# Inverses of 16 x 16 diagonal blocks on their way through memory: the transposed ones first, and by GpSimd's queue

## The chip, the cores and the metric

The kernel runs on one core of a Trainium2 chip. The metric is device time in microseconds of one execution. The core has five engines that run their own instruction streams and wait for each other by semaphores: TensorE (PE, with its weight loads as PEld), VectorE (DVE), ScalarE (ACT), GpSimd (POOL) and SyncE (SP). SP issues most transfers; ACT and POOL can issue some as well. Transfers of all queues are moved by 16 DMA engines.

## The reference

Two layers of a decoder trunk over 512 tokens of width 1024, float32. Each layer is a SwiGLU block, a mixer and a second SwiGLU block, each with a scaled residual and a layer norm. The mixer has three parts: differential attention, stick-breaking attention, and a gated delta rule with 4 heads of width 128. The change touches the delta rule only:

```python
l_mat = jnp.where(strict, jnp.einsum('bhncd,bhned->bhnce', k_beta, k) * decay, 0.0)
t_mat = l_mat + jnp.eye(CHUNK, dtype=jnp.float32)
sol = lax.linalg.triangular_solve(t_mat, rhs, left_side=True, lower=True, unit_diagonal=True)
u, w = sol[..., :dv], sol[..., dv:]
```

Per head and chunk a lower triangular matrix with ones on its diagonal is solved against; a scan over the chunks follows.

## The kernel before

Activations lie with features on the partitions and the 512 tokens along the free side. Every float32 matrix product of the projections is three matmuls of rounded parts (lines 103 to 105, `mm3`): high part of the weights by high part of x, high by low, low by high. Weights come in tiles of 512 KB (`wraw`, line 81) and are split by ScalarE (`whi`, line 89) and by VectorE or POOL (`wlo`, line 90).

The delta rule uses chunks of 128 tokens instead of the 64 of the reference, 4 chunks (NC) by 4 heads. `triangle` (line 660) makes the triangular matrices LT of a head and writes them to a scratch in memory (`scr[0]`, line 675). `base` (line 688) inverts the 16 x 16 blocks on their diagonals, all heads at once: it reads the blocks from the scratch so that each of the 128 partitions holds one whole block (U), and VectorE eliminates in 15 steps (lines 700 and 702, Y the inverse). Then Y and its transpose are written into two other scratches, each block to its place on the diagonal of a matrix that was filled with zeros at the start (line 1127, issued by POOL): `scr[1]` for the plain inverses, `scr[2]` for the transposed ones. `diagonals` (line 403) gives the addresses: 128 blocks of 16 runs of 16 numbers, 64 bytes each. From there each head's matrices come back to SBUF as whole 128 x 128 matrices, XT from `scr[1]` (line 708) and X from `scr[2]` (line 710), 256 KB each.

`double` (line 713) merges blocks of 16 into blocks of 32 for one head: a product of the masked LT with X (line 718), a copy out of PSUM by ScalarE (line 720), a product with XT (line 723), a subtraction into XT by VectorE (line 724), transposes by TensorE (line 727), and a copy into X by ScalarE (line 728). `join` goes on to 64 and 128. `outputs` (line 866) runs the scan over the chunks. Beside this chain the mixer runs attention units (`attend`, line 884; their score matmuls are lines 880 and 881, their value matmuls 909) and the projections (`full_tile`, line 345). The projection of queries and keys copies its result about in SBUF by many small transfers (`stack`, line 524, tile name `kqv`), issued by SP.

The program is written as a list of such steps; a scheduler then sets the order of the instructions on each engine from the dependencies and its own estimates of durations, so an edit in one step can move instructions of others. Each engine runs its list in order; a transfer whose data isn't ready holds up whatever stands behind it in the list of the engine that issues it.

Of the kernel before, what the change touches and what calls it, by code (L numbers as in the profile page):

```python
# [396 lines left out]
def slabs(t, h):  # L397

    a = t[:]
    return bass.AP(tensor=a.tensor, offset=a.offset + h * NC * SLAB, ap=[[P, P], [SLAB, NC], [1, P]])  # L400


def diagonals(t, h, n):

    a = t[:]
    return bass.AP(tensor=a.tensor, offset=a.offset + h * NC * SLAB, ap=[[SB * P + SB, n * NC * P // SB], [P, SB], [1, SB]])
# [20 lines left out]
def mixer(g, l):  # L427
    nc = g.nc
# [121 lines left out]
    n = 2 * HEADS  # L550
    p = pav.tile([P, T], F32, name="pt")
# [134 lines left out]
    XT, X = [None] * HEADS, [None] * HEADS  # L686

    def base(h0, n):

        q = n * NC * P // SB  # L690
        U = mp.tile([q, SB, SB], F32, name="blk")
        nc.sync.dma_start(out=U, in_=diagonals(g.scr[0], h0, n))
        Y = mp.tile([q, SB, SB], F32, name="blk")
        tt = mp.tile([q, SB * SB // 4], F32, name="blkt", bufs=1)
        nc.gpsimd.memset(Y, 0.0)
        nc.gpsimd.memset(Y.rearrange("p i j -> p (i j)")[:, 0:SB * SB:SB + 1], 1.0)
        for k in range(SB - 1, 0, -1):
            w = SB - k
            t = tt[:, 0:k * w].rearrange("p (i j) -> p i j", j=w)
            nc.vector.tensor_tensor(out=t, in0=U[:, 0:k, k:k + 1].to_broadcast([q, k, w]),  # L700
                                    in1=Y[:, k:k + 1, k:SB].to_broadcast([q, k, w]), op=ALU.mult)
            nc.vector.tensor_tensor(out=Y[:, 0:k, k:SB], in0=Y[:, 0:k, k:SB], in1=t, op=ALU.subtract)
        nc.sync.dma_start(out=diagonals(g.scr[1], h0, n), in_=Y)
        nc.vector.tensor_copy(out=U, in_=Y.rearrange("p i j -> p j i"))
        nc.sync.dma_start(out=diagonals(g.scr[2], h0, n), in_=U)
        for h in range(h0, h0 + n):
            XT[h] = mp.tile([P, NC, P], F32, name="XT", bufs=4)
            nc.sync.dma_start(out=XT[h], in_=slabs(g.scr[1], h))
            X[h] = mp.tile([P, NC, P], F32, name="inv", bufs=10)
            nc.sync.dma_start(out=X[h], in_=slabs(g.scr[2], h))  # L710


    def double(h):
# [136 lines left out]
    def triangles():  # L850

        for h in range(HEADS):
            products(h)
        norms(0, HEADS)
        for h in range(HEADS):
            triangle(h)
        base(0, HEADS)
# [401 lines left out]
```

## Time and profile before

| | |
|---|---|
| time, median of 3 runs | 2249.18 us (2244.98 to 2249.8) |
| the profiled execution | 2250.16 us, its span 2248.4 us |
| granted TensorE clock, mean | 0.985 |
| TensorE busy | 2138.2 us (95%) |
| VectorE, ScalarE, POOL busy | 1169.6, 907.9, 377.5 us |

The span goes from the first to the last instruction. A busy TensorE is not a TensorE at its peak, since matmuls are pipelined. A row of a timeline gives the start in us from the span's start, the duration, the engine, the line, the operation, output and inputs with their shapes, the count, and in brackets the idle time of the engine before it with what ended it. SPq stands for the instructions by which SP issues transfers; a transfer lands later than its issue ends.

### The profile page before, as it was taken

The page shows a single profiled execution, that of the slowest core. Times are in us where ns is not written, and L with a number is a line of the kernel's source. Part 1 is how long each engine was busy: PE and PEld are TensorE (multiplying, and loading weights), DVE is VectorE, ACT ScalarE, POOL GpSimd, SP SyncE. Part 2 cuts the span into 40 slices and gives each one's busy share as a digit, 9 for nine tenths or more (in the row PEclk, how much of TensorE's full clock was granted, in tenths as well). Part 3 has the DMA queues.
Part 4 walks back from the last instruction along what each step waited for, and adds up shares of the span by engine and source line. Part 5 has one row for each costly group of instructions (what it writes and reads, how often), then busy time and mean ns, then how long its engine had stood idle before and what let it go on. Part 6 is the DMA issues. An engine that isn't in the chain of part 4 may idle for free. (4 is left out here: it accounts for less than half of the span.)

```text
span 2248.4 us, 30132 instructions
## 1 busy us (share of the span) xinstructions
PE 2138.2 (95%) x11382; PEld 1782.6 (79%) x11382; DVE 1169.6 (52%) x2363; ACT 907.9 (40%) x1801; POOL 377.5 (17%) x327
## 2 busy tenths in 40 slices
PE   8999999999798999999999999999987989999997
PEld 7888889777677888888888888897776768888886
DVE  4533436386578833343663334263774788333426
ACT  4333324575464533332443333245753535333313
POOL 1100011426204400000130000023461234000010
PEclk9999999999899999999999999999998999999998
DMA  6423323514512233332333333234144123333322
GB/s 190 125 94 95 98 75 104 139 40 122 129 58 72 84 109 94 94 94 75 116 109 95 94 94 94 66 104 131 57 133 109 48 85 94 95 96 100 95 66 94
DMA packets 90898, 217.32 MB, mean 97 GB/s; under 512 B 21968, under 2 KB 36336, under 8 KB 90752
## 3 DMA queue, kind: packets, MB, share of 16 engines
q1 hardware_dynamic: 82848, 187.47, 27.5%
q10 hardware_dynamic: 6912, 25.17, 3.8%
q0 software_dynamic: 992, 2.75, 0.7%
q8 instruction: 90, 1.47, 0.3%
q14 instruction: 56, 0.46, 0.1%
HBM read 193.83 MB, written 6.83 MB: 89 GB/s over the span
## 5 line engine op out<-in xcount | busy, mean ns | idle before, releaser
L89 ACT CAST whi<-wraw 128x512 fp32r<-128x512 f32 x692 | 421.4, 619 | 959.4 <-PE pd L104 755.1
L90 DVE TENSOR_TENSOR wlo<-wraw,whi 128x512 fp32r<-128x512 f32 x580 | 431.0, 751 | 658.6 <-ACT whi L89 647.4
L103 PE MATMUL pd<-x,whi 128*128 128x512 f32 (+1 forms) x1920 | 726.7, 380 | 12.9 <-ACT x L1177 6.2
L105 PE MATMUL pd<-x,wlo 128*128 128x512 f32 (+1 forms) x1920 | 728.3, 380 | 3.2 <-DVE wlo L90 3.2
L104 PE MATMUL pd<-x,whi 128*128 128x512 f32 (+1 forms) x1920 | 727.7, 379 | 1.6 <-POOL x L231 1.3
L103 PEld LDWEIGHTS pd<-x,whi 128*128 128x128 f32 x1920 | 365.8, 191 | 77.5 <-ACT x L1177 6.2
L105 PEld LDWEIGHTS pd<-x,wlo 128*128 128x128 f32 x1920 | 366.2, 191 | 67.4 <-DVE wlo L90 3.4
L104 PEld LDWEIGHTS pd<-x,whi 128*128 128x128 f32 x1920 | 366.2, 191 | 66.8 <-POOL x L231 3.0
L103 PE MATMUL pd<-hhi,whi 128*128 128x512 f32 (+1 forms) x880 | 307.7, 350 | 0.0
L104 PE MATMUL pd<-hlo,whi 128*128 128x512 f32 (+1 forms) x880 | 307.7, 350 | 0.0
L105 PE MATMUL pd<-hhi,wlo 128*128 128x512 f32 (+1 forms) x880 | 307.3, 349 | 0.0
L168 POOL TENSOR_TENSOR lt<-lt 128x512 f32<-128x512 f32 x26 | 38.9, 1497 | 1065.3 <-ACT lt L165 1065.3
L103 PEld LDWEIGHTS pd<-hhi,whi 128*128 128x128 f32 x880 | 165.5, 188 | 24.4
L105 PEld LDWEIGHTS pd<-hhi,wlo 128*128 128x128 f32 x880 | 165.4, 188 | 24.1
L104 PEld LDWEIGHTS pd<-hlo,whi 128*128 128x128 f32 x880 | 165.5, 188 | 24.1
L90 POOL TENSOR_TENSOR wlo<-wraw,whi 128x512 fp32r<-128x512 f32 x112 | 150.2, 1357 | 138.7 <-ACT whi L89 70.1
L259 DVE TENSOR_TENSOR lt<-pd,lt 128x512 f32<-128x512 f32 x88 | 60.4, 689 | 111.9 <-PE pd L105 110.7
L231 POOL TENSOR_TENSOR x<-x 128x256 fp32r<-128x256 f32 x60 | 45.1, 753 | 162.5 <-ACT x L229 132.7
L134 POOL TENSOR_TENSOR x<-x 128x512 f32<-128x512 f32 x48 | 70.9, 1522 | 0.0
L261 DVE TENSOR_TENSOR hlo<-lt,hhi 128x512 fp32r<-128x512 f32 x88 | 67.0, 765 | 6.3
L165 ACT ACTIVATE lt<-x 128x256 f32<-128x256 f32 (+1 forms) x58 | 29.7, 512 | 95.8 <-DVE x L163 95.5
L568 DVE SCALAR_TENSOR_TENSOR kqv<-pd,conv,kqv 128x511 f32<-128x511 f32 (+2 forms) x72 | 53.5, 743 | 20.1 <-ACT kqv L566 18.9
(309 smaller groups left out, 2287.9 us busy)
## 6 DMA issues: line engine op xcount, KB each, us to landing
wraw<-in_w SPq DMA_DIRECT2D x308, 512.0 KB, 3.5
wraw<-in_w ACTq DMA_DIRECT2D x48, 512.0 KB, 3.6
kqv<-kqv SPq DMA_DIRECT2D x128, 64.0 KB, 2.0
kqv<-kqv SPq DMA_DIRECT2D x48, 128.0 KB, 4.7
scr<-zero POOLq DMA_DIRECT2D x2, 1032.0 KB, 11.1
x<-in_xT SPq DMA_DIRECT2D x8, 256.0 KB, 5.5
scr<-inv SPq DMA_DIRECT2D x8, 256.0 KB, 2.7
XT<-scr SPq DMA_DIRECT2D x8, 256.0 KB, 4.8
```

Source lines behind the costliest of these rows:

```text
L89: nc.scalar.copy(out=hi, in_=r)
L90: (eng or self.eng or nc.vector).tensor_tensor(out=lo, in0=r, in1=hi.bitcast(F32), op=ALU.subtract)
L103: nc.tensor.matmul(out=out, lhsT=whi, rhs=xhi, start=first, stop=False)
L104: nc.tensor.matmul(out=out, lhsT=whi, rhs=xlo, start=False, stop=False)
L105: nc.tensor.matmul(out=out, lhsT=wlo, rhs=xhi, start=False, stop=last)
L134: i = g.nc.gpsimd.tensor_tensor(out=t, in0=xhi.bitcast(F32), in1=xlo.bitcast(F32), op=ALU.add)
L165: nc.scalar.activation(out=sq[:, r], in_=t[:, r], func=AF.Square)
L168: eng.tensor_tensor(out=self.acc2[:, r], in0=self.acc2[:, r], in1=sq[:, r], op=ALU.add)
L231: eng.tensor_tensor(out=xlo[:, r], in0=t[:, r], in1=xhi[:, r].bitcast(F32), op=ALU.subtract)
L259: nc.vector.tensor_tensor(out=sg, in0=pu, in1=sg, op=ALU.mult)
L261: nc.vector.tensor_tensor(out=hlo, in0=sg, in1=hhi.bitcast(F32), op=ALU.subtract)
L568: nc.vector.scalar_tensor_tensor(out=y[:, s:], in0=p[:, :T - s], scalar=wc[:, 3 - s:4 - s], in1=y[:, s:], op0=ALU.mult, op1=ALU.add)
```

## The change

The copy that makes the transposed inverses (U) now stands ahead of both writes in the code, the transposed write comes first and is issued by POOL, and so are the four loads of X. The plain write and the four loads of XT stay on SP.

```diff
-        nc.sync.dma_start(out=diagonals(g.scr[1], h0, n), in_=Y)
         nc.vector.tensor_copy(out=U, in_=Y.rearrange("p i j -> p j i"))
-        nc.sync.dma_start(out=diagonals(g.scr[2], h0, n), in_=U)
+        nc.gpsimd.dma_start(out=diagonals(g.scr[2], h0, n), in_=U)
+        nc.sync.dma_start(out=diagonals(g.scr[1], h0, n), in_=Y)
         for h in range(h0, h0 + n):
             XT[h] = mp.tile([P, NC, P], F32, name="XT", bufs=4)
             nc.sync.dma_start(out=XT[h], in_=slabs(g.scr[1], h))
             X[h] = mp.tile([P, NC, P], F32, name="inv", bufs=10)
-            nc.sync.dma_start(out=X[h], in_=slabs(g.scr[2], h))
+            nc.gpsimd.dma_start(out=X[h], in_=slabs(g.scr[2], h))
```

After the change the copy has line 703, POOL's write 704 and SP's write 705; the loads keep 708 and 710.

In the difference below, of SP's list at the end of `base`, rows with a minus stand in the list of before, rows with a plus in the list now (of the minus rows, those from the third head on).

```order
-L708 DMA XT<-scr_99 128x4x128
-L710 DMA inv<-scr_100 128x4x128
-L708 DMA XT<-scr_99 128x4x128
-L710 DMA inv<-scr_100 128x4x128
-L524 DMA kqv<-kqv 32x512 x18
+L705 DMA scr_99<-blk 128x16x16
+L524 DMA kqv<-kqv 32x512 x3
+L708 DMA XT<-scr_99 128x4x128 x4
+L524 DMA kqv<-kqv 32x512 x17
 L81 DMA wraw<-in_w 128x1024 x153
```

The four loads of X have left SP's list, so that the four of XT follow each other, and the small copies of `stack` follow directly.

In POOL's list at the same place, with `blk` the block tile U and `inv` X:

```order
 L696 MEMSET blk 128x16
 L90 TENSOR_TENSOR wlo<-wraw,whi 128x512 x2
+L704 DMA scr_100<-blk 128x16x16
+L710 DMA inv<-scr_100 128x4x128 x4
 L995 TENSOR_TENSOR kqv<-x,kqv 128x256 x8
 L134 TENSOR_TENSOR x<-x 128x512 x8
```

The write and the loads stand behind two splits of weights and ahead of the splits of the mixer's outputs.

In TensorE's list around the first L718, the first product of `double` (`pd` is a projection's PSUM tile):

```order
 L103 MATMUL pd<-x,whi 128x512
 L104 MATMUL pd<-x,whi 128x512
+L105 MATMUL pd<-x,wlo 128x512
+L103 MATMUL pd<-x,whi 128x512
+L104 MATMUL pd<-x,whi 128x512
+L105 MATMUL pd<-x,wlo 128x512
+L103 MATMUL pd<-x,whi 128x512
 L718 MATMUL pa<-inv,lt 128x128 x4
-L105 MATMUL pd<-x,wlo 128x512
-L103 MATMUL pd<-x,whi 128x512
-L104 MATMUL pd<-x,whi 128x512
-L105 MATMUL pd<-x,wlo 128x512
```

Five matmuls of a projection have moved from behind L718 to ahead of it; further on the order of the doubling and the attention units differs in many places.

## Rows read from the trace of the kernel before

**Rows 1.** The page, its head.
```profile
span 2248.4 us, 30132 instructions
```

**Rows 2.** The waits: waiting engine and line, releaser; us, times, longest.
```profile
PE pa L718 <- DMA inv<-scr: 8.2, 2, 4.8
```

**Rows 3.** The timeline of SP's issues, layer 0, end of `base`.
```profile
593.89 0.37 SPq L703 DMA_DIRECT2D scr<-blk  x1
594.37 0.88 SPq L705 DMA_DIRECT2D scr<-blk  x1
...
597.86 0.53 SPq L708 DMA_DIRECT2D XT<-scr  x1
598.49 0.48 SPq L710 DMA_DIRECT2D inv<-scr  x1
...
603.31 11.93 SPq L524 DMA_DIRECT2D kqv<-kqv  x18
```

**Rows 4.** The timeline of VectorE, the same place.
```profile
593.86 0.37 DVE L704 COPY blk<-blk 128x256 f32<-128x256 f32 x1
594.15 0.68 DVE L511 SCALAR_TENSOR_TENSOR kqv<-pd,kqv 128x512 fp32r<-128x512 f32 x1
605.93 0.69 DVE L90 TENSOR_TENSOR wlo<-wraw,whi 128x512 fp32r<-128x512 f32 x1 [11.10 <-ACT whi L89]
```

**Rows 5.** The chain that ended last, layer 1: start, us, what.
```profile
1707.84 4.03 DMA scr<-blk
```

**Rows 6.** The timeline of TensorE, layer 0, around the first L718.
```profile
601.92 2.04 PE L718 MATMUL pa<-inv,lt 128*128 128x128 f32 x8 [3.36 <-DMA inv<-scr]
603.61 0.77 PE L105 MATMUL pd<-x,wlo 128*128 128x512 f32 x1
604.18 0.63 PE L103 MATMUL pd<-x,whi 128*128 128x512 f32 x1
604.61 0.63 PE L104 MATMUL pd<-x,whi 128*128 128x512 f32 x1
...
606.47 1.13 PE L723 MATMUL pa<-XT,inv 128*128 128x128 f32 x8
```

**Rows 7.** The timeline of TensorE, layer 1, the same place.
```profile
1715.30 2.05 PE L718 MATMUL pa<-inv,lt 128*128 128x128 f32 x8 [4.80 <-DMA inv<-scr]
...
1720.98 1.20 PE L723 MATMUL pa<-XT,inv 128*128 128x128 f32 x8
```

**Rows 8.** The timeline of TensorE, layer 0, later heads.
```profile
613.04 1.06 PE L718 MATMUL pa<-inv,lt 128*128 128x128 f32 x8
613.85 0.42 PE L880 MATMUL psc<-kqv 128*128 128x384 f32 x1
...
617.26 1.06 PE L718 MATMUL pa<-inv,lt 128*128 128x128 f32 x8
```

**Rows 9.** The timeline of ScalarE, layer 0.
```profile
605.28 0.62 ACT L89 CAST whi<-wraw 128x512 fp32r<-128x512 f32 x1 [12.33 <-PE pd L104]
605.80 0.58 ACT L720 COPY inv<-pa 128x512 f32<-128x512 f32 x1
```

**Rows 10.** The page's transfers: issuer, count, KB each, median us from issue to landing.
```profile
scr<-zero POOLq DMA_DIRECT2D x2, 1032.0 KB, 11.1
...
inv<-scr SPq DMA_DIRECT2D x8, 256.0 KB, 5.2
...
scr<-blk SPq DMA_DIRECT2D x4, 128.0 KB, 3.5
...
lt<-in_mask POOLq DMA_DIRECT2D x1, 128.0 KB, 2.3
```

**Rows 11.** The timeline of POOL, the second zero fill.
```profile
53.26 1.13 POOL L1127 DMA_DIRECT2D scr<-zero  x1 [11.51 <-issue]
```

**Rows 12.** The timeline of POOL after 593.8, layer 0.
```profile
665.83 1.56 POOL L995 TENSOR_TENSOR kqv<-x,kqv 128x256 fp32r<-128x256 f32 x2 [72.03 <-ACT kqv L994]
```

**Rows 13.** Stretches: us, engines' busy time, granted clock, DMA share, GB/s.
```profile
602.00:603.00 1.00, 1.00 (x5) 1.00 (x6) 0.00 (x0) 0.00 (x0) 0.00 (x0) 0.50 1.11 300
```

More of the change, by code (lines that the diff above doesn't have):

```diff
@@ L702, in base @@
             nc.vector.tensor_tensor(out=Y[:, 0:k, k:SB], in0=Y[:, 0:k, k:SB], in1=t, op=ALU.subtract)
+        nc.vector.tensor_copy(out=U, in_=Y.rearrange("p i j -> p j i"))
+        nc.gpsimd.dma_start(out=diagonals(g.scr[2], h0, n), in_=U)
         nc.sync.dma_start(out=diagonals(g.scr[1], h0, n), in_=Y)
-        nc.vector.tensor_copy(out=U, in_=Y.rearrange("p i j -> p j i"))
-        nc.sync.dma_start(out=diagonals(g.scr[2], h0, n), in_=U)
         for h in range(h0, h0 + n):
```

## The prediction

> **What bounds the kernel now.** First the page's head: the span is 2248.4 us [rows 1]. The profiled execution took 2250.16 us, so 1.76 us lie around the span; the median of the three runs shown is 2249.18, 0.98 below this execution. The sum is made against 2250.16 and the 0.98 is taken off at the end.
>
> Second, the view of waits: TensorE waits 8.2 us in all, in two places and at most 4.8 us, for the transfer "inv<-scr", which is X of head 0 (line 710) [rows 2]. These two places, one in each layer, are where the change works. Third, the timelines around the first. VectorE ends the copy into U at 594.23 and SP issues its write at 594.37 [rows 3, 4]. That write lands 4.03 us after its issue (row of layer 1) [rows 5], in layer 0 at 598.40; SP issues the load of X at 598.49 [rows 3], and TensorE starts the first product of `double` (L718) at 601.92, after 3.36 us without work [rows 6]. In layer 1 L718 starts at 1715.30 after 4.80 us [rows 7].
>
> After that a chain sets the pace: L718, ScalarE's copy L720, L723, VectorE's subtraction L724, L727, and the next head. The L718 of two successive heads stand 4.22 us apart (613.04 and 617.26) [rows 8]. So what counts is when the first L723 can start: 606.47 and 1720.98, that is 4.55 and 5.68 us after L718 [rows 6, 7]. In between TensorE does nine matmuls of the projection, and ScalarE's L720 stands behind a cast that waits until 605.28 for a TensorE matmul (L104), ending a wait of 12.33 us [rows 9].
>
> **The change part by part.**
>
> *Swapped order and the copy first.* VectorE's instructions keep their order: in the kernel before, the copy already stood directly behind the last L702, and the plain write was issued beside it. Cost 0. What the copy's write gains is that it no longer stands behind the plain write on SP: 594.37 less 594.23 is 0.14 us, and some of this is the signal. I take 0.05. The load gains as little: SP had issued it 0.09 us after the landing (598.49 less 598.40). SP's issue time, 0.37 and 0.53 us for the two instructions ahead [rows 3], was thus almost all hidden.
>
> In sentences of their own: the Trainium skill, "DMA: Bandwidth & Descriptors", section "Issuing engines are not separate DMA queues", says that several issuing engines save only the time of issuing. Going by that rule alone the move is worth at most these 0.23 us a layer; the trace agrees as far as it shows the issue hidden.
>
> *The write by POOL's queue (128 x 16 runs of 64 bytes).* No row shows this write on POOL. Low end: the plain write, first in its queue, lands after about 3.0 us (the page's median for the four writes is 3.5 [rows 10], and the second is at 4.0); lower still would be POOL's load of 128 KB in 2.3 us [rows 10], which has few runs. High end: POOL's zero fill, also 128 x 16 runs but of 516 bytes, landed after 11.1 us (median of two) [rows 10]; its issue took 1.13 us [rows 11]. Between 2.3 and 11.1 I take 4.2: the same bytes at the same addresses are SP's 3.0, POOL's issue is longer by about 0.8 (1.13 less 0.37), and the two writes now run side by side where they ran one behind the other, 0.4 more. POOL is free: its last subtraction (L90) ends at 593.8 and the next work before was at 665.83, after 72.03 us of idling [rows 12], so what stands behind the POOL transfers (L995) does not feel them. The write then lands at 594.32 plus 4.2, 598.5, against 598.40: 0.1 late.
>
> In sentences of their own: VectorE runs L511 from 594.15 to 594.83, over the start of POOL's issue, and then nothing until 605.93 [rows 4]. The Trainium skill, "SBUF — State Buffer", section "SBUF: two separate sides", warns that a VectorE instruction in a two-port mode locks GpSimd out, so that it cannot write descriptors and its DMA starts late; it gives 3.1 us against 0.62 beside a copy. Whether L511 is such an instruction no run here shows. If it is, the lock ends with it: 0.5 us a layer, and the gain of the sum below would be 1.0 smaller.
>
> *The load by POOL's queue.* Before, from issue to L718 3.43 us (598.49 to 601.92) [rows 3, 6], behind one XT load. Now all four XT loads, 1 MB, go out on SP from about 597, as soon as the plain write has landed. At the 300 GB/s of the busy stretch [rows 13] they fill 3.5 us, to about 601.5, and X of head 0, issued at 598.6, shares the engines with the last two. Low end 2.3 (POOL's 128 KB load [rows 10]); high end 5.2 (the median of the eight X loads, most of them issued behind others) [rows 10]. I take 3.6, near the row before, since before it also shared. X arrives at 602.2 instead of 601.9: about 0.3 late, 0.6 for two layers.
>
> *The order of TensorE.* The scheduler now puts five matmuls of the projection, 13 instead of 8, ahead of L718, and leaves four instead of nine between L718 and L723. The five find TensorE idle: at 0.43 each (604.18 to 604.61 [rows 6]) they are 2.15 us, inside the 3.36 and 4.80 us of waiting. The cast that L720 stands behind then runs before L718, because the matmul that it waits for is among the five (it was the third after L718). New distance L718 to L723, at the slow clock of this stretch (granted 0.50 from 602 to 603, that is 1.2 GHz [rows 13]): 1.69 to the next matmul (601.92 to 603.61), then 0.57 and three times 0.43, together 3.55. ScalarE's L720 needs 0.58 of this and is hidden; if that cover goes, L720 and its handoff add up to 0.6. Gain: 4.55 less 3.55 is 1.00 in layer 0, 5.68 less 3.55 is 2.13 in layer 1, together 3.1. The same 17 matmuls are done at L723 as before, so nothing is only put off to there.
>
> *What follows.* XT of head 0 is issued about a microsecond earlier than 597.86 and is needed last at L723: no cost. The copies of keys and queries behind the loads on SP (L524, 18 of them from 603.31 [rows 3]) start about 3 us earlier. TensorE's order of the doubling changes, too, but that stretch is paced by the chain of 4.22 us; later the attention work already used as filler is missing. I take 0 for all this, with 3 us either way.
>
> **The sum.** Less 3.1, plus 0.6: less 2.5 us. 2250.16 becomes 2247.7, and by the 0.98 a median of 2246.7.
>
> **The rivals.**
>
> *Slower: POOL's write of 2048 small runs lands late.* For it: the only POOL transfer with as many runs took 11.1 us, and a second one like it did not start its issue until 11.51 us after the first [rows 11]. Against: it carried eight times the bytes, beside weight loads. Every microsecond that the write lands later than assumed delays L718, and all behind it, once a layer. With 10 us instead of 4.2 it is 2 x 5.8 less 2.5, or 9.1 slower: 2258.3. It decides from (2.5 + 4.5) / 2 above 4.2, so a landing after 7.7 us is slower than a measurement's doubt; at 5.4 us the gain is gone.
>
> *Faster: the clock stays up.* Before, L718 took 1.69 us to the next matmul at 1.2 GHz and later 0.81 (613.04 to 613.85 [rows 8]), about half; the matmuls' 0.43 would be 0.22. With the wait shortened by five matmuls TensorE may come to L718 at 2.4 GHz: 0.88 plus 4 x 0.21, some 1.7 a layer, 3.4 in all: 2243.3. Against: in layer 1 2.6 us or more of the wait stay.
>
> *Faster, by transfers: POOL's write and load land like its plain loads.* The 2.3 us of [rows 10] instead of 4.2 and 3.6 is 3.2 us a layer; X cannot be used before TensorE is through with its 13 matmuls (598.56, where the wait of 3.36 began, plus 2.15 is 600.7), so 1.5 us a layer count: 3.0 in all, 2243.7. In a sentence of its own: the Trainium skill, "DMA: Bandwidth & Descriptors", section "Anatomy of one DMA — SWDGE (gpsimd) path", fits a DMA by 2.0 us plus its bytes at 436 GB/s, which agrees with the 2.3 but not with the 11.1 of the zero fill (it would give 4.4).
>
> *No effect: the gain is lost behind.* The fill-in work that now stands ahead of L718 is missing in the stretch of the state scan, and the chain's lead is eaten there: 2249.
>
> **How the numbers follow.** About 0.2% of the time, 4.5 us, is what a measurement of this kernel tells from no change. Chances: forecast 0.32, lost behind 0.18, slow write 0.23, clock 0.16, fast transfers 0.11. The forecast (less 2.5) and the loss (0) lie within 0.2%; a little of the forecast's spread of 3 us goes beyond on the fast side, and the two fast rivals lie 5.5 to 5.9 below and just beyond the bound. So faster 0.30, same 0.46, slower 0.24. The range goes from both fast rivals together (2240) to close to the slow write (2257).
>
> **What would show it.** Right: in the profile after, 13 matmuls ahead of L718, the wait before L718 down to some 1.5 us in layer 0 (598.56 plus 2.15 is 600.7, X at 602.2), L723 about 3.6 us behind L718, and POOL's write landing some 4 us after its issue. Wrong: a landing above 6 us, a wait before L718 as long as before or longer, or the same time of L723 and then more idling of TensorE between 608 and 700 us.

## The result, and the profile after

The changed kernel takes 2276.26 us (median of 6 runs, 2272.78 to 2284.49) against 2249.46 for the kernel before (6 runs): a ratio of 1.0125 over the runs (1.0119 by the two medians), 95% interval 1.0112 to 1.0138. It is 26.8 us slower by the medians. 2246.7 was forecast, with a range of 2240 to 2257. The profiled execution is the slowest of the six (2284.49), so lengths of stretches are compared here, not times from the start. Its head answers to [rows 1]:

```profile
span 2282.7 us, 30147 instructions
```

The waits (us, times, longest). The first row answers to [rows 2]; the second is ScalarE's copy of a scan step's result out of PSUM, 22.4 us in all and at most 4.0 before:

```profile
PE pa L718 <- DMA inv<-scr: 14.2, 2, 8.0
ACT o L840 <- PE pa L798: 50.7, 12, 15.7
```

The place that the prediction was about, layer 0, answers to [rows 3, 4 and 6]: VectorE's copy, the issues of SP and POOL, and TensorE.

```profile
595.69 0.38 DVE L703 COPY blk<-blk 128x256 f32<-128x256 f32 x1
595.72 0.37 SPq L705 DMA_DIRECT2D scr<-blk  x1
596.49 1.22 POOL L704 DMA_DIRECT2D scr<-blk  x1 [0.86 <-DVE blk L703]
598.72 2.66 SPq L708 DMA_DIRECT2D XT<-scr  x4
601.75 2.99 POOL L710 DMA_DIRECT2D inv<-scr  x4 [4.04 <-DMA scr<-blk]
607.95 2.04 PE L718 MATMUL pa<-inv,lt 128*128 128x128 f32 x8 [8.00 <-DMA inv<-scr]
611.50 1.86 PE L723 MATMUL pa<-XT,inv 128*128 128x128 f32 x8
```

POOL issues the first load of X only at 601.75, three microseconds after SP began to issue the four loads of XT, and L718, which waits for X, starts 6.2 us later. The wait before L718 is 8.0 us, although five more matmuls stand ahead of it. L723 follows after 3.55 us, as forecast. Layer 1 answers to [rows 7]:

```profile
1740.30 2.05 PE L718 MATMUL pa<-inv,lt 128*128 128x128 f32 x8 [6.17 <-DMA inv<-scr]
1743.85 1.48 PE L723 MATMUL pa<-XT,inv 128*128 128x128 f32 x6
```

That is some 4 us a layer, less what L718 to L723 gives back. The greater part lies further on, in the state scan (L779 is a product of each of its steps, with XT and the scaled values). Lengths read from the timelines of TensorE and VectorE, layer 0 / layer 1, in us, start to start:

| from, to | before | after |
|---|---|---|
| copy, first L718 | 8.06 / 7.95 | 12.26 / 12.05 |
| first L718, first L723 | 4.55 / 5.68 | 3.55 / 3.55 |
| first L723, last L738 (doubling and joins) | 35.7 / 35.8 | 35.9 / 36.3 |
| last L738, first L779 | 10.70 / 10.70 | 14.30 / 14.30 |
| first L779, last L779 (scan) | 34.24 / 34.21 | 41.64 / 41.80 |

The differences add up to 14.5 and 13.7 us. Between the last L738 and the scan TensorE now does attention units first that stood inside the scan before. The two ends of the scan in layer 0, first before, then after:

```profile
652.84 0.66 PE L779 MATMUL pa<-inv,XT 128*128 128x128 f32 x4
...
687.08 0.67 PE L779 MATMUL pa<-inv,XT 128*128 128x128 f32 x4
```

```profile
661.72 0.49 PE L779 MATMUL pa<-inv,XT 128*128 128x128 f32 x2
...
703.36 0.68 PE L779 MATMUL pa<-inv,XT 128*128 128x128 f32 x4
```

In the scan, POOL in layer 0 after the change:

```profile
673.71 4.31 POOL L995 TENSOR_TENSOR kqv<-x,kqv 128x256 fp32r<-128x256 f32 x6 [4.38 <-ACT kqv L994]
677.96 9.83 POOL L134 TENSOR_TENSOR x<-x 128x512 f32<-128x512 f32 x8
```

and VectorE in the same stretch:

```profile
674.19 0.69 DVE L814 TENSOR_REDUCE oms<-lt 128x4 f32<-128x512 f32 x1 [0.31 <-ACT lt L810]
...
675.13 0.16 DVE L815 SCALAR_TENSOR_TENSOR oms<-oms,sq 128x4 f32<-128x4 f32 x1
675.32 0.67 DVE L816 TENSOR_SCALAR oms<-oms 128x4 f32<-128x4 f32 x1
...
682.97 1.18 DVE L114 TENSOR_TENSOR orr_t<-of 128x4 f32<-128x4 f32 x1
684.18 1.19 DVE L115 SCALAR_TENSOR_TENSOR orr_t<-orr_t,oms 128x4 f32<-128x4 f32 x1
...
686.62 1.19 DVE L818 TENSOR_TENSOR of<-of,sqs 128x4 f32<-128x4 f32 x1
687.73 0.34 DVE L775 SCALAR_TENSOR_TENSOR inv<-pa,neG,inv 128x128 f32<-128x128 f32 x1
...
690.03 0.16 DVE L114 TENSOR_TENSOR orr_t<-of 128x4 f32<-128x4 f32 x1
```

The operations on 128 x 4 numbers belong to the norm of the scan's output (`emit`, line 801, with the inverse square root of lines 111 to 116). Alone they take 0.16 us. Beside POOL's splits L995, 0.72 each (4.31 by 6), they take up to 0.67, and beside its residual additions L134, 1.23 each (9.83 by 8), up to 1.19: most of these small operations last about as long as one POOL instruction. The additions begin 16.2 us after the first L779 (677.96 less 661.72); before, they began 25.6 us after it (678.43 less 652.84), when the norm of the first two chunks was all but done. Behind them in VectorE's list stands L775, the next step of the scan, and TensorE waits for it:

```profile
680.79 0.71 PE L773 MATMUL pa<-S,kqv 128*128 128x128 f32 x4 [3.15 <-DVE S L792]
688.22 0.76 PE L779 MATMUL pa<-inv,XT 128*128 128x128 f32 x2 [5.49 <-DVE inv L775]
```

The stretches (busy us of PE, PEld, DVE, ACT, POOL; granted clock; DMA share; GB/s) show the clock's part: from 682 to 688 TensorE was busy for 0.73 us, and in the following 4 us its granted clock was 0.54, hardly above the lower of its two levels (1.2 GHz).

```profile
682.00:688.00 6.00, 0.73 (x2) 0.00 (x1) 5.86 (x7) 0.00 (x0) 5.79 (x5) 0.50 0.00 0
688.00:692.00 4.00, 3.78 (x12) 3.19 (x13) 2.16 (x9) 0.00 (x0) 0.00 (x0) 0.54 0.02 6
692.00:696.00 4.00, 4.00 (x29) 3.37 (x28) 3.40 (x15) 1.21 (x3) 0.00 (x0) 1.00 0.00 0
```

### The profile page after: what moved, and what is told of

Read it like the earlier page. It is cut to its first block, busy times and chain, and to the rows that moved or that the text cites. A ratio compares the mean times of both kernels' runs of the same rounds, so it can differ in the third digit from the quotient of the medians.

```text
span 2282.7 us, 30147 instructions
## 1 busy us (share of the span) xinstructions
PE 2148.6 (94%) x11382; PEld 1789.9 (78%) x11382; DVE 1189.7 (52%) x2363; ACT 906.9 (40%) x1801; POOL 385.4 (17%) x337
## 4 chain that ended last, share of the span: by engine, by line
PE 75%; DVE 14%; DMA 4%; ACT 3%; issue 2%; POOL 1%; ACTq 0%; SPq 0%; POOLq 0%; DVEq 0%
PE pd L104 22%; PE pd L105 22%; PE pd L103 22%; DMA wraw<-in_w 3%; DVE wlo L90 1%; PE po L909 1%; ACT whi L89 1%; DVE at L939 1%; POOL wlo L90 1%; DVE x L212 1%; DVE x L220 1%; PE psc L880 1%; PE pt L904 1%; DVE kqv L568 1%; DVE x L163 1%
## 5 line engine op out<-in xcount | busy, mean ns | idle before, releaser
L134 POOL TENSOR_TENSOR x<-x 128x512 f32<-128x512 f32 x48 | 70.2, 1510 | 0.0
```

The costliest lines, as they stand in the source:

```text
L134: i = g.nc.gpsimd.tensor_tensor(out=t, in0=xhi.bitcast(F32), in1=xlo.bitcast(F32), op=ALU.add)
```

## The experiments

Theory O: the scheduler's new order, not the later X, costs most. Rival T: the later X costs it and the order only follows. Medians of the kernel before lie between 2248.1 and 2250.0 beside these runs; ratios are to it, with 95% intervals.

**Order and transfers taken apart.** A table gives, for TensorE, VectorE and ScalarE, the sequence that the other kernel's scheduler chose in the stretch where the two differ (the same permutation in both layers), and holds it by dependencies without waits:

```diff
         program(ctx, tc, a, out, mixer)
+        pin(tc)
+def pin(tc):
...
+            row = [per[eng][base + i + j] for i, n in table for j in range(n)]
+            for x, y in zip(row, row[1:]):
+                tc.add_manual_dep(y, x.name, mybir.DependencyInfo(mybir.DependencyClass.NoSync, mybir.DependencyReason.DATA), reason="order")
```

> The changed kernel's transfers with the kernel before's order of TensorE, VectorE and ScalarE in the stretch where the two differ. Theory O (the new order costs most of the 27 us): 2257 us (2252 to 2262), since only the lateness of X is left, some 4 us per layer. Rival T (the later transfers cost it, and the order only follows them): 2276 us (2270 to 2282).

> The kernel before's transfers, all on SP, with the changed kernel's order of TensorE, VectorE and ScalarE in the same stretch. Theory O: 2268 us (2262 to 2274), the scan starting some 3.5 us later after the last L738 and taking some 7 us more in each layer although X comes as early as before. Rival T: 2249 us (2246 to 2253).

The changed transfers in the old order: 2258.54 us, 1.0046 (1.0033 to 1.0059). The old transfers in the new order: 2274.07 us, 1.0111 (1.0097 to 1.0125). So by the medians the order alone costs 25 us, the transfers alone 10, both together 27: theory O, and the two do not add. TensorE's two ends of the scan in layer 0, first the changed transfers in the old order:

```profile
657.33 0.66 PE L779 MATMUL pa<-inv,XT 128*128 128x128 f32 x4
...
691.56 0.68 PE L779 MATMUL pa<-inv,XT 128*128 128x128 f32 x4
```

then the old transfers in the new order:

```profile
657.31 0.49 PE L779 MATMUL pa<-inv,XT 128*128 128x128 f32 x2
...
698.94 0.68 PE L779 MATMUL pa<-inv,XT 128*128 128x128 f32 x4
```

34.23 and 41.63 us: the length of the scan goes with the order, whenever X came.

**What in the order makes the scan long.** `emit` keeps its last scaling (L819) in a list, and POOL's additions wait for the last of them:

```diff
-        nc.vector.tensor_tensor(out=o, in0=o, in1=last(ff, P), op=ALU.mult)
+        ended.append(nc.vector.tensor_tensor(out=o, in0=o, in1=last(ff, P), op=ALU.mult))
...
-        nm.residual(d)
+        nm.residual(d, ended[-1], True)
```

> The changed kernel with the eight residual additions on POOL (L134) made to wait for the last output scaling of the state scan (L819), order of all engines unchanged. Theory C, inside O (the small VectorE operations of the output norm are slowed by POOL's additions beside them, and that stretches the scan): the 128x4 operations fall from 0.6 to 1.2 us to about 0.17 except where L995 still runs, and the time is 2266 us (2261 to 2272). Rival (the scan is long for another reason, such as the order of its steps): 2276 us (2272 to 2281).

> The same edit on the kernel before, as a control. Theory C: only a few small operations stood beside POOL's additions there, so 2247 us (2243 to 2250); the rival: 2249 us (2246 to 2252).

The changed kernel: 2273.88 us, 1.0118 (1.0102 to 1.0133); the kernel before: 2265.08 us, 1.0070 (1.0058 to 1.0083). Both times missed their theory, and the first lies in the rival's range. But the scan of the changed kernel fell from 41.6 to 32.1 us with the order of all engines unchanged, while that of the kernel before stayed at 34.2. What was gained was paid behind: there the additions now stand beside VectorE's gate products L1025 and splits L995. In the changed kernel the time from the last L779 of layer 0 to the copy of layer 1 is 1027.7 us with this edit, against 1020.6 with the additions at the moment chosen further below. VectorE in the kernel before with this edit:

```profile
699.60 3.37 DVE L1025 TENSOR_TENSOR x<-x,kqv 128x512 f32<-128x512 f32 x2 [1.52 <-ACT x L827]
702.89 5.71 DVE L995 TENSOR_TENSOR kqv<-x,kqv 128x256 fp32r<-128x256 f32 x4
```

Without POOL beside them these took 0.68 and 0.42 each. So the additions were left out, and then put at another moment:

```diff
+        i = g.nc.sync.dma_start(out=t, in_=xhi.bitcast(F32)) if dma else g.nc.gpsimd.tensor_tensor(out=t, in0=xhi.bitcast(F32), in1=xlo.bitcast(F32), op=ALU.add)
...
-        nm.residual(d)
+        nm.residual(d, dma=True)
```

> The changed kernel with the mixer's eight residual additions on POOL left out: a transfer on SP copies the high part alone, so the low part of the residual is missing from the sum; the order of all engines is the changed kernel's. Theory C: the state scan (first to last L779) takes about 32 us instead of 41.7 and nothing is paid behind it, so 2257 us (2252 to 2262). Rival (the waits of the scan have another cause than POOL's additions): 2272 to 2278 us.

2259.48 us, 1.0051 (1.0039 to 1.0064): theory C, the scan takes 32.1 us. With all additions there again, waiting for the second L819 instead of the last (`ended[1]`), in the changed kernel and in the old transfers with the new order held:

> The changed kernel with POOL's eight residual additions made to wait for the second output scaling of the state scan (L819) instead of the last, so that they run beside scan steps of VectorE that read PSUM (L775, L781, L792: unslowed beside additions in the kernel before); nothing is left out, and the order of all engines is the changed kernel's. Theory C: first to last L779 about 32 us and nothing paid behind, 2259 us (2255 to 2263), what leaving the additions out gave. Rival (any VectorE operation pays beside the additions, wherever they stand): 2268 to 2276 us.

> The kernel before's transfers with the changed kernel's order held, and the additions made to wait for the second L819. What is left of the order alone is then attention ahead of the scan, 3.6 us per layer from the last L738 to the first L779. Theory: 2274 less 17 is 2257 us (2253 to 2261), and the 2 to 3 us between this run and the one with the changed kernel's transfers are all that the later X costs once TensorE has more to do in the meantime. Rival (X late and the order together cost more than their parts): the gap between the two runs is 8 to 10 us, as with the kernel before's order.

The first: 2260.02 us, 1.0041 (1.0026 to 1.0057), theory C again. It is the place of the additions that costs, not their amount. TensorE's two ends of the scan in layer 0:

```profile
660.30 0.49 PE L779 MATMUL pa<-inv,XT 128*128 128x128 f32 x2
...
692.40 0.68 PE L779 MATMUL pa<-inv,XT 128*128 128x128 f32 x4
```

Beside the additions VectorE now runs scan steps that read PSUM:

```profile
684.23 9.93 POOL L134 TENSOR_TENSOR x<-x 128x512 f32<-128x512 f32 x8 [7.62 <-DVE o L819]
...
684.28 0.61 DVE L775 SCALAR_TENSOR_TENSOR inv<-pa,neG,inv 128x128 f32<-128x128 f32 x2 [0.19 <-PE pa L773]
685.50 0.42 DVE L781 TENSOR_TENSOR vn<-pa,brk 128x256 f32<-128x256 f32 x1 [0.61 <-PE pa L779]
686.73 0.61 DVE L792 SCALAR_TENSOR_TENSOR S<-S,eG,pa 128x128 f32<-128x128 f32 x2 [0.81 <-PE pa L786]
```

These keep their length (0.30, 0.42 and 0.30 each). The kernel before had its additions (from 678.43) beside such steps by chance of its order.

The second: 2252.45 us, 1.0010 (1.0001 to 1.0020), below its forecast. Without the clash the new order costs hardly anything: the scan starts 3.6 us later and takes 2.1 us less. The gap of 7.6 us to the run before it is what the later X costs, close to the rival's 8 to 10; 2 to 3 us were forecast. In steps of one change each, the loss is thus 2.5 us for the order, 7.6 for the later X, and 16.2 for the additions beside the small operations (2276.26 less 2260.02). The shares depend on the order of the steps: with the old transfers the additions cost 21.6 us (2274.07 less 2252.45). In the scan itself the clash takes 9.5 to 10.6 us a layer with either transfers.

**Why X is late.** Parts of the change alone, in the kernel before's order:

> Only the write of the transposed inverses on POOL's queue; the loads of X stay on SP; the order of TensorE, VectorE and ScalarE is held to the kernel before's. Theory (the lateness of X of some 4.2 us per layer is shared by write and loads, 1.6 to 2 for the write): the first L718 comes about 2 us later after the copy than before (about 10.0 us instead of 8.0) and the time is 2253 us (2250 to 2256). Rival (the loads carry it all): 8.0 us and 2249 us; or the write carries it all: 12.2 us and 2258 us.

> Only the loads of X on POOL's queue; both writes stay on SP, the transposed ones first; the order of TensorE, VectorE and ScalarE is held to the kernel before's. Theory: the first L718 about 2.5 us later after the copy than before (10.5 us instead of 8.0) and 2254 us (2251 to 2257). Rivals: the loads carry all of it, 12.2 us and 2258 us; or none of it, 8.0 us and 2249 us.

The write alone: 2249.61 us, 0.9999 (0.9988 to 1.0011), L718 8.5 / 8.4 us behind the copy. The loads alone: 2246.12 us, 0.9983 (0.9972 to 0.9994), L718 after 7.8 / 7.6 us. Both missed their theory, since neither part alone delays X as it does beside the other (12.4 and 12.1 us with both, in the same order). The loads alone, layer 0:

```profile
597.44 3.02 POOL L710 DMA_DIRECT2D inv<-scr  x4 [4.03 <-DMA scr<-blk]
598.49 2.53 SPq L708 DMA_DIRECT2D XT<-scr  x4
...
601.30 2.05 PE L718 MATMUL pa<-inv,lt 128*128 128x128 f32 x8 [4.68 <-DMA inv<-scr]
```

Here X is issued ahead of XT and lands after 3.86 us; in the changed kernel it is issued behind and lands after 6.2. If that is the cause, XT put behind X on POOL's queue must cure it with the late write left as it is:

```diff
-            XT[h] = mp.tile([P, NC, P], F32, name="XT", bufs=4)
-            nc.sync.dma_start(out=XT[h], in_=slabs(g.scr[1], h))
             X[h] = mp.tile([P, NC, P], F32, name="inv", bufs=10)
             nc.gpsimd.dma_start(out=X[h], in_=slabs(g.scr[2], h))
+        for h in range(h0, h0 + n):
+            XT[h] = mp.tile([P, NC, P], F32, name="XT", bufs=4); nc.gpsimd.dma_start(out=XT[h], in_=slabs(g.scr[1], h))
```

> The changed kernel with the four loads of XT put on POOL's queue too, behind the four of X, order of TensorE, VectorE and ScalarE held to the kernel before's. Theory B (with the write 2 us late, SP's loads of XT are issued ahead of X's and X's bytes queue behind theirs): X's first load lands in 3.9 us instead of 6.4, the first L718 stands about 9.9 us behind the copy instead of 12.2, and the time is 2254 us (2251 to 2257) against 2258.5 with XT on SP. Rival (a load behind a write on POOL's queue is slow by itself): 12.2 us and 2258 to 2262 us.

SP, POOL and TensorE in layer 0 (line 708 is now the load of X, 710 that of XT):

```profile
594.33 12.20 SPq L524 DMA_DIRECT2D kqv<-kqv  x17
599.73 2.99 POOL L708 DMA_DIRECT2D inv<-scr  x4 [3.90 <-DMA scr<-blk]
602.72 2.97 POOL L710 DMA_DIRECT2D XT<-scr  x4
603.61 2.04 PE L718 MATMUL pa<-inv,lt 128*128 128x128 f32 x8 [5.22 <-DMA inv<-scr]
```

X lands in 3.88 us and L718 stands 9.8 / 10.0 us behind the copy, as expected; 2251.03 us, 1.0012 (1.0001 to 1.0023), against 2258.54 with XT on SP. SP's small copies (L524) are issued all through the load of X here, so they are not what made it late. Write and loads of X on ScalarE's queue instead of POOL's, with XT on SP again:

> The changed kernel with write and loads on ScalarE's queue instead of POOL's, order of TensorE and VectorE held to the kernel before's. Theory Q (it is POOL's queue that is slow, not a second queue): landings as on SP, some 3.5 us for the write and at most 4 us for the first load, so that X is no later than before and the time is 2248 us (2244 to 2251). Rival (a second queue slows both, whichever engine issues, or ScalarE's copies are held up behind the waits of its issues): X 1 to 4 us late per layer, 2252 to 2260 us.

2253.31 us, 1.0012 (1.0001 to 1.0023), L718 after 10.1 / 9.5 us. Theory Q fell: the write takes 4.4 us there (4.6 to 5.0 on POOL, 3.5 for the two on SP), its load of X is issued at 599.11 behind SP's of XT at 598.35, and L718 starts 5.3 us later. So POOL's queue is only a part of it; the second place behind XT is the other.

**The order left free, and two attempts to gain.** The loads alone, without the table:

> The loads of X on POOL's queue, both writes on SP, as in the run with only the loads moved, but with the order left to the scheduler, which again puts attention ahead of the scan (782 lines of difference on TensorE against the kernel before). Theory O: the held order gave 2246 us, the free one adds the 25 us that the order alone cost, 2271 us (2266 to 2276). Rival (the new order costs only where X comes late): 2246 to 2252 us.

2268.51 us, 1.0096 (1.0082 to 1.0109): theory O. Here X comes as early as in the held run (7.7 us), and the scheduler's order alone makes 22 us of difference.

> Only the loads of X on POOL, with five more projection matmuls ahead of the first L718 on TensorE than in the run with only the loads moved (the scheduler's order for the kernel with only the write moved, held); scan and attention in the kernel before's order. Theory: TensorE idles 4.7 us ahead of L718 there, the five fill 2.1 us of it and are saved behind: 2243 us (2240 to 2247) against 2246. Rival (the doubling is a chain of copies and waits in which the five were hidden): 2246 us (2244 to 2249).

2246.48 us, 0.9991 (0.9982 to 1.0001): the rival held, no gain shows in the time. In layer 0 L723 follows L718 after 3.5 us instead of 5.7, in layer 1 after 4.6 instead of 4.4, since there it waits for XT, which with X first comes second:

```profile
1715.54 1.13 PE L718 MATMUL pa<-inv,lt 128*128 128x128 f32 x8 [2.13 <-DMA inv<-scr]
...
1720.10 1.13 PE L723 MATMUL pa<-XT,inv 128*128 128x128 f32 x8 [0.90 <-DMA XT<-scr]
```

> The kernel before with the mixer's eight residual additions on VectorE instead of POOL (the rest of the order is left to the scheduler; some 170 lines of it change in the scan and behind it). Theory C (POOL's additions slow VectorE's operations beside them, and cost more there than they take): 2245 us (2240 to 2249), the additions taking about 0.69 us each on VectorE. Rival (VectorE is the bound in the scan, and 8 times 0.69 us are paid in full in each layer): 2255 to 2260 us.

2249.88 us, 0.9998 (0.9987 to 1.0009): the additions take 0.69 us each on VectorE, the scan is 1.7 to 1.9 us longer, and nothing is gained or lost. Theory and rival both missed. The best version is the one with the loads alone on POOL and the order held, 0.17% faster than the kernel before.

## Why the prediction was wrong

*Swapped order and the copy first (a gain of 0.05).* Too small: in the run with the loads alone POOL can issue 4.0 us behind the start of the copy (593.48 to 597.44); before, SP issued the load of X 4.6 us behind it. This is 0.7 us a layer, of which POOL's longer load (3.9 us against 3.4) takes most back.

*POOL's write (4.2 us, X's data 0.1 late).* Mis-sized: 5.0 us, and POOL's issue begins 0.42 us behind the end of the copy (596.07 to 596.49). POOL issues the load of X 6.1 us behind the copy's start, against SP's 4.6 before: 1.4 us late. The landing after 5.0 us is short of the 7.7 at which the rival of the slow write was to decide. How much of it goes to L511, which runs on VectorE at the same time, no run separates.

*POOL's load (3.6 us).* Mis-sized, and this is the larger term: 6.2 us. The working had X share the DMA engines with the last two loads of XT (its sum has a slip: 597 plus 3.5 is 600.5, not 601.5). With the load issued 1.3 us later than assumed all four go ahead. Issued ahead of XT, POOL's load takes 3.9 us, so the estimate of the queue itself was near. "Transposed first" was undone by the two queues: what is issued first is now settled by which write lands first.

*TensorE's order around L718 (3.55 us between L718 and L723, a gain of 3.1).* Right to the hundredth: 3.55 in both layers, 1.00 and 2.13 us gained there. Some of it goes back at once: L723 itself now runs at a granted clock of 0.56 in layer 0, 1.86 us against 1.13, and the stretch from it to the last L738 is 0.2 to 0.5 us longer. The rival of the clock fell: from L718 to the next matmul it is 1.70 us, as before, so after its wait of 8.0 us TensorE still comes to it at the lower level. Its mechanism did show where X came early with the same matmuls ahead: in the run with five more matmuls ahead (waits of 2.2 and 2.1 us) L718 ran at a granted clock of 1.00 in both layers, 0.88 us to the next matmul; no gain showed in the time.

*What follows (0, with 3 us either way).* This is the step that failed. The new order behind L718 costs 3.6 us ahead of the scan and 7.4 to 7.6 in it, in each layer. The prediction had seen that the order differs in many places, and costed it at nothing because the doubling is paced by its chain. That was true of the doubling (35.7 us before, 35.9 after in layer 0), but the zero was carried over to the scan, of which it shows no row, and VectorE's list was taken as unchanged. The rival "no effect: the gain is lost behind" named the right place, the state scan, but as a loss of cover on TensorE and with a size of 2.5 us. The real mechanism is another: the norm of the scan's output now falls beside POOL's additions. Rows for it stood in the trace before: beside POOL's last two splits L818 takes 0.65 us instead of 0.16, and L819 1.19 instead of 0.69; POOL's first addition, which overlaps the end of L819, takes 1.72.

```profile
677.16 0.65 DVE L818 TENSOR_TENSOR of<-of,sqs 128x4 f32<-128x4 f32 x1
677.74 0.74 POOL L995 TENSOR_TENSOR kqv<-x,kqv 128x256 fp32r<-128x256 f32 x1
677.84 1.19 DVE L819 TENSOR_TENSOR o<-o,of 128x512 f32<-128x512 f32 x1
678.43 1.72 POOL L134 TENSOR_TENSOR x<-x 128x512 f32<-128x512 f32 x1
678.96 0.59 DVE L775 SCALAR_TENSOR_TENSOR inv<-pa,neG,inv 128x128 f32<-128x128 f32 x2
```

The Trainium skill, "SBUF — State Buffer", section "SBUF: two separate sides", says that VectorE (in a two-port mode, or with two inputs in SBUF) and GpSimd share one pair of ports as a lock that is held for a whole instruction, and that the loser waits for all of it. The trace agrees: 1.19 us beside additions of 1.23, 0.67 beside splits of 0.72, and operations with an operand in PSUM, or with one input as in L814, untouched. Operations on one tensor and constants (L816, L111) were slowed as well; whether they run in a two-port mode no row shows. The prediction drew on this section for POOL's transfers, where it priced the lock at 0.5 us a layer, and not for POOL's arithmetic.

What stays open: why the scheduler's estimates turn the order over when the loads go to POOL and leave it when only the write does, and why by the medians the later X costs 7.6 us in the order with the clash removed, 10 in the old order, and only 2.2 in the changed one (2276.26 less 2274.07). From the copy to the last L779, both layers together, the profiled executions do not show this: there the later X adds 8.8, 9.0 and 8.3 us, and the order alone 19.9, so that in this stretch the two nearly add (28.1 for both). What differs lies outside it, or in the spread of the few runs.

As a test the prediction had named a wait before L718 as long as before or longer: that one showed it wrong (8.0 us), the one on the write's landing (above 6 us) did not.

## What to carry to other kernels

Where a scheduler sets the order, moving a transfer to another queue can change the whole order behind it, as it did here: cost the moved instructions stretch by stretch, or hold the old order and change the transfer alone. Before trusting that a second queue brings something earlier, ask which of the two queues will issue its loads first. Look up what POOL's arithmetic runs beside: small VectorE operations in a chain can pay about one POOL instruction each (0.67 and 1.19 us here instead of 0.16).

## What was not expected of the hardware

- Eleven VectorE operations on 128 x 4 numbers, about 0.16 us each alone, took 11.1 us beside POOL between 676 and 688 (L111, L114 to L116, L818), and with them the scan was 9.5 us longer. A 128 x 512 sum over SBUF (L814) kept its 0.69 beside L995, at 674.19.
- Of two sets of four loads of 256 KB the one issued earlier, by 0.8 to 3 us, landed first, whichever queue it was on: L718 starts 3.9 us after the issue of the first X where X goes ahead of XT, 5.3 (X on ACT's queue) or 6.2 (on POOL's) where it goes behind.
- Of two writes of 2048 runs of 64 bytes the later one took longer on a queue of its own (4.4 us on ACT beside 3.6 on SP, 5.0 on POOL beside 3.0 on SP) than as the second of two on SP (4.0).
